# Rooms for the loads of "products down", and modulation rows, transposes and pairs of blocks further apart in a two-layer hybrid transformer step

## Chip, cores and metric

The kernel runs on one core of one Trainium2 chip. The metric is device time of one execution in microseconds, the median of the runs shown. The core's engines are PE (TensorE, matmuls and transposes), DVE (VectorE), ACT (ScalarE), POOL (GpSimd) and SP (SyncE, which here issues every DMA from one queue, in order). Each engine works through its own instructions in order and waits on semaphores where another engine or a DMA must have finished first.

## What is computed

One inference step of two layers over 1024 latent tokens and 128 context tokens, that is nine blocks of 128 tokens (0 to 7 latent, 8 the prompt), width 1024. Layer 0 has differential attention, layer 1 windowed attention with a sink; each is followed by a SwiGLU feed-forward of width 2816 = 22 x 128. Norms and modulation stand around each part:

```python
for i in range(DEPTH):
    mp = modulation(c_ctx[None, :], w_mod[i], b_mod[i])      # shift, scale, gate, twice, for the prompt
    ms = modulation(c, w_mod[i], b_mod[i])                   # and for the latent tokens
    hs = pre_norm_modulate(xs, norm_g[i, 0], ms[0], ms[1])
    ...                                                      # attention -> ys
    xs = post_norm_residual(xs, ys, norm_g[i, 1], ms[2])
    hs = pre_norm_modulate(xs, norm_g[i, 2], ms[3], ms[4])
    xs = post_norm_residual(xs, swiglu(hs, w_gate[i], w_up[i], w_down[i]), norm_g[i, 3], ms[5])
```

## The kernel before

Every product is made in three matmuls on values split into a high and a low part (hi x hi, hi x lo, lo x hi). So each weight and each activation is first split: ACT rounds it into the high part, DVE subtracts to get the low part.

A layer runs in stages: projections of q, k and v (`Qkv`), attention, output projection with the norms (`OProj`), "products up" (`Ffn.up`, the gate and up weights by a Strassen-like scheme in sums B11 to T4, accumulators X, Y and Z), and "products down" (`Ffn.downs`). After that comes the next layer's projection.

SBUF space is handed out as rooms of 128 x 1024 floats. `Rooms` is a list of free rooms: `take` removes the first, `give` appends at the end, and `retire` takes rooms out for good. A tile laid into a room waits until the reads and writes of the tile before it are done. H are 18 rooms on the left (h0 to h17), L nine more (ten in layer 1), D 18 on the right (d0 to d17). In layer 0 the rooms H become, pair by pair, the transposed input hT of layer 1's projections, two rooms per block.

Products down goes in steps (g, d): three groups g of three blocks, and 22 slices d of w_down, 66 steps in all, numbered 0 to 65 as loads. A step is 18 matmuls (dacc). `load_w` runs three steps ahead (lead = 3); in each step it takes five rooms and gives two back at once:

```python
x, a = rooms.take(name="fraw"), rooms.take(name="araw")
...
h, lo, ahl = [rooms.take((P, D), F32R, name) for name in ("fh", "fl", "ahl")]
...
rooms.give(x, a)
```

The three rooms of h, lo and ahl come back after the step's matmuls. For layer 0 the list starts as H[0:12], what is free of L and D[16:18]; at (0, 8) `retire(H)` takes all of H out of it. Beside the products, `mod_tasks_lean` makes modulation rows in these steps (DVE sums macc over eight pieces wmod of w_mod; then ACT and DVE split it to mhl; then `out()` has PE reduce it to a row, mrow, and DVE reads that row), and the blocks of the group before go through their norms (`norm`, parts 0 to 3 at d = 1 to 12), are stored to x_d, and are transposed (`turn`, at d = 12, 14, 16) into hT. In the last group the first projection weights of layer 1 (w2: wraw, split to whi and wlo) are loaded.

In products up, `mod_tasks_lean` runs in the same way between the products, and the mrow tile uses a "u" bank of PSUM, of which there are two; accumulator Z uses them too, for its two parts.

`pair` transposes two normed blocks xn on PE into the two "u" banks each (tp_n), copies the first (ACT B11h, B21h, DVE raw) and makes the sums from the second. Two pairs stand in `OProj` after block steps 5 and 6, the others in the first slice of products up, after products 0, 2 and 4 of part 0 (list `late`).

PE, DVE, ACT and POOL run in the order in which the code is written (`manual_schedule`); the order of DMAs on SP is set by a scheduler.

Of the kernel before, what the change touches and what calls it, by code (L numbers as in the profile page):

```python
# [18 lines left out]
P = 128  # L19
# [25 lines left out]
def hybrid_step(ctx: ExitStack, tc: tile.TileContext, x_prompt, x_sample, cache_diff_k, cache_diff_v,  # L45
# [201 lines left out]
    def mod_tasks_lean(ps, tasks, mroom, rooms, rows):  # L247

        out, n = None, 0
        for l, j, half in [(*t, half) for t in tasks for half in range(2)]:  # L250
# [3 lines left out]
            for kb in range(KB):  # L254
# [12 lines left out]
                if kb == 0 and out:  # L267
                    out()
# [1098 lines left out]
    class Halves:  # L1367
# [57 lines left out]
        def pair(self, part, c, xs, rooms):  # L1425

            raws, n = [], P if len(xs) == 2 else P // 2
            for i, x in enumerate(xs):
                tps = self.turned(x)
                if i == 0:  # L1430
                    raws.append(new(rooms[0], [P, 2, 4, n], F32, "raw"))
                    self.first(part, c, [tp[:, :, 0:n] for tp in tps], raws[0])
                if i == len(xs) - 1:
                    raws += [new(r, [P, 2, 4, n], F32, "raw") for r in rooms[1:]]
                    self.second(part, c, [tp[:, :, P - n:P] if n < P else tp for tp in tps], raws)

# [4 lines left out]
    class Ffn:  # L1441
# [127 lines left out]
        def up(self, tasks, mroom, late, pt, ahead):  # L1569

            self.pt = pt
            gen = mod_tasks_lean(self.ps, tasks, mroom, self.rooms, junk)
# [71 lines left out]
        def downs(self, mods, yx, hT, ahead=()):  # L1644
# [4 lines left out]
            for i, (g, d) in enumerate(steps):  # L1649
# [12 lines left out]
                if g:  # L1662
# [5 lines left out]
                    if self.l == 0 and d in (12, 14, 16):  # L1668
                        self.turn(GROUPS[g - 1][(d - 12) // 2])
# [3 lines left out]
                if g == 2 and d == 17:  # L1673
# [57 lines left out]
    class Layer:  # L1731
# [8 lines left out]
        def begin(self, stack):  # L1740
# [15 lines left out]
            def pair(part, c, *tbs):  # L1756
                rooms = [where[f"x{OORDER.index(tb) % 5}"] for tb in tbs]
                f.hv.pair(part, c, [op.xn[tb] for tb in tbs], [*rooms, *self.temps][:3])
                if part:
                    f.rooms.free += rooms  # L1760

            self.pair = pair
            for k, c, tbs in (((5, 1), 0, (0, 4)), ((6, 1), P, (1, 5))):
                hooks.setdefault(k, []).append(lambda c=c, tbs=tbs: pair(0, c, *tbs))
            hooks[5, 1].insert(0, lambda: f.hv.lay(0, iter(H)))
# [33 lines left out]
        def ffn(self, tasks):  # L1799

            l, f, op, H = self.l, self.f, self.op, self.H
            with ExitStack() as high:
# [3 lines left out]
                for tag in names:  # L1806
# [7 lines left out]
                late = [[lambda: self.pair(1, 0, 2, 6), lambda: f.fetch(1)], (), [lambda: self.pair(1, P, 3, 7)], (),  # L1814
                        [lambda: self.pair(1, 2 * P, TB_PROMPT)]]
# [10 lines left out]
        def down(self, stack, ahead=lambda ring: {}, tasks=()):  # L1826
# [4 lines left out]
            yx, cut = R[0:6], R[6:16] if l == 0 else R[6:8]  # L1831
# [3 lines left out]
            self.ring = Ring(cut[0:2], cut[2:] + rest + yx)  # L1835
            f.rooms.free += [r for r in self.old.free if r not in H] + rest
            steps = ahead(self.ring)
            if l == 0:

                steps.setdefault((0, 8), []).append(lambda: f.rooms.retire(H))  # L1840
                spare = Rooms(cut[4:6])
                gen = mod_tasks_lean(self.ps, tasks, [cut[0], *cut[1:4]], spare, new(cut[6]))
# [4 lines left out]
            self.low.close()  # L1847

# [144 lines left out]
```

## Time and profile before

| what | value |
|---|---|
| median of 3 runs | 3303.95 us (3297.66 to 3308.42) |
| the profiled execution's own time | 3303.71 us |
| its span, first to last instruction | 3301.9 us |
| mean granted TensorE clock | 0.969 |
| PE busy | 3038.3 us, 92% |
| DVE, ACT, POOL busy | 2023.9, 1423.1, 1359.9 us |

A share of busy time is an average over all stages; what ends a wait in one stage is read from the windows and waits of that stage. The granted clock is a share of full speed. "idle <- X" names what ended an engine's wait.

### The profile page before, as it was taken

Reading aid. Unit: us, or ns where it says so; the run is one execution under the profiler, and the core shown is the slowest. Engines: PE = TensorE matmul, PEld = TensorE weight load, DVE = VectorE, ACT = ScalarE, POOL = GpSimd, SP = SyncE. Lnnn points to the kernel's source line nnn. Section 1 sums busy time; section 2 is a strip of 40 time slices with the busy share of each in tenths; the row PEclk is TensorE's granted clock in tenths of the full one; section 3 lists DMA queues with packets and bytes.
Section 4 is the critical chain, followed back from the end, with each engine's and each line's share of the span. In section 5 each row is a group of like instructions: output and inputs, shape, how many; then the busy total and the mean of one; then the engine's idle time right before and its main releaser. Section 6 shows DMA issues by size and latency. Waiting matters only on the chain.

```text
span 3301.9 us, 47896 instructions
## 1 busy us (share of the span) xinstructions
PE 3038.3 (92%) x17998; PEld 2652.1 (80%) x17998; DVE 2023.9 (61%) x2789; ACT 1423.1 (43%) x2764; POOL 1359.9 (41%) x1186
## 2 busy tenths in 40 slices
PE   8999889888969999999868899899996999999999
PEld 5888777777758999998656678777776999998887
DVE  6776388887566777735563453799666733334454
ACT  6332267776543333333333422677444333333442
POOL 2543399997333434440010054466433433431001
PEclk9999999999989999999989899999998999999999
DMA  6765533332422333327454434443432422225564
GB/s 212 211 214 182 194 111 114 117 112 82 147 90 89 112 115 116 118 65 251 158 175 136 154 120 137 135 129 105 123 107 84 119 72 69 81 77 191 179 206 148
DMA packets 373808, 442.23 MB, mean 134 GB/s; under 512 B 26804, under 2 KB 295644, under 8 KB 373576
## 3 DMA queue, kind: packets, MB, share of 16 engines
q1 hardware_dynamic: 373576, 439.16, 42.4%
q8 instruction: 142, 2.33, 0.3%
q14 instruction: 90, 0.74, 0.1%
HBM read 335.71 MB, written 103.37 MB: 133 GB/s over the span
## 4 chain that ended last, share of the span: by engine, by line
PE 40%; DVE 8%; DMA 5%; ACT 4%; issue 1%; POOL 1%; ACTq 0%; SPq 0%; DVEq 0%; POOLq 0%
DMA fraw<-in_w_down_dram 5%; PE guX L1516 4%; PE guX L1518 4%; PE guX L1517 4%; PE dacc L1633 3%; PE dacc L1634 3%; PE dacc L1635 3%; DVE fl L1618 2%; PE guY L1518 2%; PE guY L1516 2%; PE guY L1517 2%; ACT fh L1617 2%; PE qacc L555 1%; PE qacc L556 1%; PE qacc L557 1%
## 5 line engine op out<-in xcount | busy, mean ns | idle before, releaser
L1633 PE MATMUL dacc<-fh,ahl 128*128 128x512 f32 x792 | 320.4, 405 | 24.5 <-ACT ahl L1619 14.6
L1618 DVE TENSOR_TENSOR fl<-fraw,fh 128x1024 fp32r<-128x1024 f32 x132 | 168.1, 1274 | 251.9 <-ACT fh L1617 251.8
L1634 PE MATMUL dacc<-fl,ahl 128*128 128x512 f32 x792 | 317.9, 401 | 3.6 <-DVE fl L1618 3.5
L1635 PE MATMUL dacc<-fh,ahl 128*128 128x512 f32 x792 | 317.5, 401 | 0.0
L1549 POOL TENSOR_TENSOR sg<-sg,U 128x256 f32<-128x256 f32 x88 | 75.0, 852 | 573.7 <-ACT sg L1548 558.4
L1617 ACT CAST fh<-fraw 128x1024 fp32r<-128x1024 f32 x132 | 138.4, 1049 | 339.4 <-DMA fraw<-in_w_down_dram 324.4
L154 POOL TENSOR_TENSOR xt<-yacc,xt 128x1024 f32<-128x1024 f32 (+1 forms) x19 | 46.3, 2439 | 534.6 <-DVE yacc L153 282.3
L555 PE MATMUL qacc<-whi,hh 128*128 128x512 f32 x648 | 261.5, 404 | 0.9 <-ACT hh L430 0.9
L556 PE MATMUL qacc<-wlo,hh 128*128 128x512 f32 x648 | 255.8, 395 | 0.0
L557 PE MATMUL qacc<-whi,hl 128*128 128x512 f32 x648 | 255.8, 395 | 0.0
L783 POOL TENSOR_TENSOR aT<-a,aT 128x512 fp32r<-128x512 f32 x186 | 240.1, 1291 | 15.5
L743 DVE TENSOR_REDUCE nm<-S 128x1 f32<-128x1280 f32 x128 | 190.3, 1486 | 50.4 <-PE S L736 50.1
L1633 PEld LDWEIGHTS dacc<-fh,ahl 128*128 128x128 f32 x792 | 153.1, 193 | 65.5 <-ACT ahl L1619 20.4
L736 PE MATMUL S<-K,q 128*128 128x512 f32 (+1 forms) x768 | 182.4, 373 | 12.8 <-ACT e L748 8.6
L1634 PEld LDWEIGHTS dacc<-fl,ahl 128*128 128x128 f32 x792 | 152.9, 193 | 41.5 <-DVE fl L1618 8.1
L265 DVE SCALAR_TENSOR_TENSOR macc<-wmod,sc,macc 128x512 f32<-128x512 f32 x196 | 184.2, 983 | 1.0 <-DMA wmod<-in_w_mod_dram 1.0
L1635 PEld LDWEIGHTS dacc<-fh,ahl 128*128 128x128 f32 x792 | 152.6, 193 | 38.5 <-DVE ahl L1620 4.0
L748 ACT ACTIVATE e<-S,nm 128x1280 f32<-128x1280 f32 x128 | 171.5, 1340 | 4.5 <-DVE nm L743 4.5
L577 ACT CAST xT<-tpx 128x512 fp32r<-128x512 f32 x127 | 68.4, 591 | 239.2 <-issue 125.3
L736 PEld LDWEIGHTS S<-K,q 128*128 128x128 f32 x768 | 135.7, 190 | 43.4 <-ACT e L748 19.1
L1488 DVE TENSOR_TENSOR fl<-fsum,fh 128x1024 fp32r<-128x1024 f32 x84 | 102.6, 1221 | 99.3 <-ACT fh L1486 99.3
L110 POOL TENSOR_SCALAR aT<-a 128x512 fp32r<-128x512 f32 x192 | 152.3, 793 | 21.8 <-ACT a L772 21.8
(369 smaller groups left out, 9710.7 us busy)
## 6 DMA issues: line engine op xcount, KB each, us to landing
fraw<-in_w_down_dram SPq DMA_DIRECT2D x132, 512.0 KB
wmod<-in_w_mod_dram SPq DMA_DIRECT2D x112, 256.0 KB
araw<-a_d SPq DMA_DIRECT2D x132, 192.0 KB
fraw<-in_w_gate_dram SPq DMA_DIRECT2D x44, 512.0 KB
fraw<-in_w_up_dram SPq DMA_DIRECT2D x42, 512.0 KB
qT_d<-xT SPq DMA_DIRECT2D x36, 512.0 KB
q<-qT_d SPq DMA_DIRECT2D x64, 256.0 KB
wraw<-in_w_qkv_diff_dram SPq DMA_DIRECT2D x24, 512.0 KB
```

The lines of the kernel that those rows point to most:

```text
L555: pe.matmul(acc, lhsT=xh, rhs=hi[:, a, :], start=(kb == 0), stop=False)
L556: pe.matmul(acc, lhsT=xh, rhs=lo[:, a, :], start=False, stop=False)
L557: pe.matmul(acc, lhsT=xl, rhs=hi[:, a, :], start=False, stop=(kb == KB - 1))
L736: pe.matmul(S[:, j:j + n], lhsT=self.q[:, f, m, i * P:(i + 1) * P], rhs=kv[self.h][0][:, m, j:j + n], start=(f == 0), stop=(f == 1))
L783: (dve if self.last else pool).tensor_tensor(out=lo, in0=x, in1=hi.bitcast(F32), op=ALU.subtract)
L1516: pe.matmul(o, lhsT=hi[:, kb, :], rhs=xh[:, kb, :], start=(first and kb == 0), stop=False, **more)
L1517: pe.matmul(o, lhsT=hi[:, kb, :], rhs=xl[:, kb, :], start=False, stop=False, **more)
L1617: act.copy(out=h, in_=x)
L1618: dve.tensor_tensor(out=lo, in0=x, in1=h.bitcast(F32), op=ALU.subtract)
L1633: pe.matmul(acc, lhsT=ah, rhs=hi[:, cs], start=(d == 0), stop=False)
L1634: pe.matmul(acc, lhsT=ah, rhs=lo[:, cs], start=False, stop=False)
L1635: pe.matmul(acc, lhsT=al, rhs=hi[:, cs], start=False, stop=(d == NDF - 1))
```

## The change

It has five parts, in the diff's order. `mod_tasks_lean` gets a number, lag: `out()` of one half row comes after piece lag of the next half instead of piece 0 (1 in products up, 3 in products down). `Halves.pair` becomes a generator that pauses after each block; in `OProj` its two halves come after the first and the second half projection of steps 5 and 6 (before, both after the second), and in the first slice of products up after products 1, 2, 3, 4 and 6. The turns move from d = 12, 14, 16 to 15, 17, 19, and the prompt's modulation rows from (2, 17) to (2, 20). Two rooms of D go from the ring of the next weights to the loads; the ring's raw rooms are H[15:17] during the stage and those two D rooms after it. H[0:6] are retired at (1, 12) and H[6:12] at (2, 4), in place of all H at (0, 8).

```diff
--- before.py
+++ after.py
@@ -244,7 +244,8 @@
             rows_out(l, j, half * 512, 512, r, *pre)
             yield
 
-    def mod_tasks_lean(ps, tasks, mroom, rooms, rows):
+    def mod_tasks_lean(ps, tasks, mroom, rooms, rows, lag):
+
 
         out, n = None, 0
         for l, j, half in [(*t, half) for t in tasks for half in range(2)]:
@@ -264,7 +265,7 @@
                     else:
                         dve.scalar_tensor_tensor(out=a, in0=w, scalar=sc[:, kb, cd:cd + 1], in1=a, op0=ALU.mult,
                                                  op1=ALU.add)
-                if kb == 0 and out:
+                if kb == lag and out:
                     out()
                 yield
             pre = rows_in(iter([rows[0:2, i * 512:(i + 1) * 512] for i in range(2)]), l, j, half * 512, 512)
@@ -1433,6 +1434,7 @@
                 if i == len(xs) - 1:
                     raws += [new(r, [P, 2, 4, n], F32, "raw") for r in rooms[1:]]
                     self.second(part, c, [tp[:, :, P - n:P] if n < P else tp for tp in tps], raws)
+                yield
 
 
 
@@ -1569,7 +1571,7 @@
         def up(self, tasks, mroom, late, pt, ahead):
 
             self.pt = pt
-            gen = mod_tasks_lean(self.ps, tasks, mroom, self.rooms, junk)
+            gen = mod_tasks_lean(self.ps, tasks, mroom, self.rooms, junk, 1)
             for d in range(NDF):
                 if d == 0:
 
@@ -1665,12 +1667,12 @@
                         part, j = [int(x) for x in NORMS[d - 1]]
                         if part < 2 or self.l == 0:
                             self.norm(part, GROUPS[g - 1][j])
-                    if self.l == 0 and d in (12, 14, 16):
-                        self.turn(GROUPS[g - 1][(d - 12) // 2])
+                    if self.l == 0 and d in (15, 17, 19):
+                        self.turn(GROUPS[g - 1][(d - 15) // 2])
                 if d == 17:
                     for j in range(3):
                         self.load_x(GROUPS[g][j], j)
-                if g == 2 and d == 17:
+                if g == 2 and d == NDF - 2:
                     self.mod(TB_PROMPT)
             for j in range(3):
                 for d in range(NDF - self.nlast, NDF):
@@ -1755,14 +1757,17 @@
 
             def pair(part, c, *tbs):
                 rooms = [where[f"x{OORDER.index(tb) % 5}"] for tb in tbs]
-                f.hv.pair(part, c, [op.xn[tb] for tb in tbs], [*rooms, *self.temps][:3])
+                yield from f.hv.pair(part, c, [op.xn[tb] for tb in tbs], [*rooms, *self.temps][:3])
                 if part:
                     f.rooms.free += rooms
+                yield
 
             self.pair = pair
-            for k, c, tbs in (((5, 1), 0, (0, 4)), ((6, 1), P, (1, 5))):
-                hooks.setdefault(k, []).append(lambda c=c, tbs=tbs: pair(0, c, *tbs))
-            hooks[5, 1].insert(0, lambda: f.hv.lay(0, iter(H)))
+            hooks.setdefault((5, 0), []).append(lambda: f.hv.lay(0, iter(H)))
+            for i, c, tbs in ((5, 0, (0, 4)), (6, P, (1, 5))):
+                steps = pair(0, c, *tbs)
+                for half in range(2):
+                    hooks.setdefault((i, half), []).append(lambda steps=steps, n=1 + half: step(steps, n))
 
             def room(tag, shape, dt, name):
                 return new(where[tag], shape, dt, name)
@@ -1811,8 +1816,9 @@
                 R.tile([P, 512], F32, name="room", tag="mw", bufs=2)
                 self.temps = [macc, (R, "mw", 2)]
                 pt = high.enter_context(sbuf(f"pt{l}", "right"))
-                late = [[lambda: self.pair(1, 0, 2, 6), lambda: f.fetch(1)], (), [lambda: self.pair(1, P, 3, 7)], (),
-                        [lambda: self.pair(1, 2 * P, TB_PROMPT)]]
+                pairs = [self.pair(1, c, *tbs) for c, tbs in ((0, (2, 6)), (P, (3, 7)), (2 * P, (TB_PROMPT,)))]
+                late = [[], [lambda: step(pairs[0])], [lambda: step(pairs[0], 2), lambda: f.fetch(1)],
+                        [lambda: step(pairs[1])], [lambda: step(pairs[1], 2)], [], [lambda: step(pairs[2], 2)]]
 
                 def switch():
 
@@ -1828,23 +1834,25 @@
 
             l, f, H = self.l, self.f, self.H
             R = ring_rooms(stack.enter_context(sbuf(f"D{l}", "right")), [f"d{i}" for i in range(18)])
-            yx, cut = R[0:6], R[6:16] if l == 0 else R[6:8]
+            yx, cut = R[0:6], R[6:14] if l == 0 else R[6:8]
             mods = [H[12:15], H[15:18]] if l == 0 else [cut[0:1], cut[1:2]]
             hT = alloc_hT(H) if l == 0 else None
             rest = [r for r in R[6:] if r not in cut]
-            self.ring = Ring(cut[0:2], cut[2:] + rest + yx)
+            self.ring = Ring(H[15:17], cut + rest[2:] + yx)
             f.rooms.free += [r for r in self.old.free if r not in H] + rest
             steps = ahead(self.ring)
             if l == 0:
 
-                steps.setdefault((0, 8), []).append(lambda: f.rooms.retire(H))
+                steps.setdefault((1, 12), []).append(lambda: f.rooms.retire(H[0:6]))
+                steps.setdefault((2, 4), []).append(lambda: f.rooms.retire(H[6:12]))
                 spare = Rooms(cut[4:6])
-                gen = mod_tasks_lean(self.ps, tasks, [cut[0], *cut[1:4]], spare, new(cut[6]))
+                gen = mod_tasks_lean(self.ps, tasks, [cut[0], *cut[1:4]], spare, new(cut[6]), 3)
                 for i in range(2 * NDF):
                     steps.setdefault(divmod(i, NDF), []).append(lambda: next(gen, None))
             with tc.manual_schedule(engines=ENGINES):
                 f.downs(mods, yx, hT, steps)
             self.low.close()
+            self.ring.rooms = rest[0:2], self.ring.rooms[1]
 
     before0, before1 = ExitStack(), ExitStack()
     with psum("gp0") as ps, sbuf("hT0", "left") as hp, sbuf("wq0", "left") as wq:
```

Three places show how instructions stand. First SP's queue in the last group of layer 0's products down (w_down into fraw, the a values into araw, stores to x_d), with the semaphores that each DMA waits for. Before:

```order
L1715 DMA x_d<-xt 128x1024 [waits Pool_49]
L1614 DMA fraw<-in_w_down_dram 128x1024 [waits DMAHW2_49,DVE_49]
L1615 DMA araw<-a_d 128x384 [waits DMAHW6_49,DMAHW3_49,DVE_49]
L1614 DMA fraw<-in_w_down_dram 128x1024 [waits DMAHW5_49,DVE_49]
L1615 DMA araw<-a_d 128x384 [waits DMAHW6_49,DVE_49]
```

And now:

```order
L1717 DMA x_d<-xt 128x1024 [waits DMAHW2_49,Pool_49]
L1616 DMA fraw<-in_w_down_dram 128x1024 [waits DMAHW3_49,PE_49]
L1617 DMA araw<-a_d 128x384 [waits DMAHW4_49,DVE_49,PE_49]
L1616 DMA fraw<-in_w_down_dram 128x1024 [waits DMAHW5_49,DVE_49,PE_49]
L1617 DMA araw<-a_d 128x384 [waits DMAHW6_49,DVE_49,PE_49]
```

The load of w_down waited for DVE alone (its room was last a raw tile, which DVE read); now it waits for PE too (its room was last a split weight).

Second, PE in products up of layer 0 (guX, guZ and guY are the accumulators, mrow the modulation row). Before:

```order
L1516 MATMUL guX<-B11h,fh 128x320
L1517 MATMUL guX<-B11l,fh 128x320
L1518 MATMUL guX<-B11h,fl 128x320
L279 MATMUL mrow<-mhl,sel 2x512 x4
L1516 MATMUL guZ<-B21h,fh 128x256
L1517 MATMUL guZ<-B21l,fh 128x256
```

And now:

```order
L1518 MATMUL guX<-T2h,fh 128x320
L1519 MATMUL guX<-T2l,fh 128x320
L1520 MATMUL guX<-T2h,fl 128x320
L280 MATMUL mrow<-mhl,sel 2x512 x4
L1518 MATMUL guY<-T3h,fh 128x256
L1519 MATMUL guY<-T3l,fh 128x256
```

The row's four matmuls moved from just ahead of Z to behind the second X product, ahead of Y.

Third, DVE in step 5 of layer 0's output projection (xn are normed blocks, L137 the reciprocal root of the norm, tp_n the transposed block, raw its copy). Before:

```order
L137 RECIPROCAL rs<-ss 128x1
L153 SCALAR_TENSOR_TENSOR xn<-oacc,rs,q 128x512 x2
L137 RECIPROCAL rs<-ss 128x1
L145 SCALAR_TENSOR_TENSOR xn<-K,rs,bc 128x1024
L146 TENSOR_TENSOR xn<-xn,bc 128x1024
L1395 COPY raw<-tp_n 128x512 x2
L1411 TENSOR_TENSOR raw<-tp_n,raw 128x512
```

And now:

```order
L1396 COPY raw<-tp_n 128x512 x2
L1278 RECIPROCAL rs_9227<-ss_9161 128x8
L1279 TENSOR_TENSOR rs_9227<-rs_9227,r_9160 128x8
L137 RECIPROCAL rs<-ss 128x1
L153 SCALAR_TENSOR_TENSOR xn<-oacc,rs,q 128x512 x2
L137 RECIPROCAL rs<-ss 128x1
L145 SCALAR_TENSOR_TENSOR xn<-K,rs,bc 128x1024
L146 TENSOR_TENSOR xn<-xn,bc 128x1024
L1412 TENSOR_TENSOR raw<-tp_n,raw 128x512
```

The copies of the pair's first block moved ahead of the norm of block step 4; the sums with the second block stay behind it.

## Rows read from the trace of the kernel before

**Rows 1.** The page: busy time of PE, and the chain's shares by line.

```profile
PE 3038.3 (92%) x17998; PEld 2652.1 (80%) x17998; DVE 2023.9 (61%) x2789; ACT 1423.1 (43%) x2764; POOL 1359.9 (41%) x1186
...
DMA fraw<-in_w_down_dram 5%; PE guX L1516 4%; PE guX L1518 4%; PE guX L1517 4%; PE dacc L1633 3%; PE dacc L1634 3%; PE dacc L1635 3%; DVE fl L1618 2%; PE guY L1518 2%; PE guY L1516 2%; PE guY L1517 2%; ACT fh L1617 2%; PE qacc L555 1%; PE qacc L556 1%; PE qacc L557 1%
```

**Rows 2.** Windows: us, busy PE PEld DVE ACT POOL, clock, DMA share, GB/s.

```profile
1512.60:1571.40 58.80, 58.36 (x265) 47.90 (x264) 40.12 (x55) 22.29 (x31) 2.68 (x2) 1.00 0.76 258
1571.40:1894.80 323.40, 259.17 (x1015) 196.24 (x1014) 159.04 (x200) 110.48 (x171) 28.64 (x12) 0.89 0.48 156
3050.00:3250.00 200.00, 200.00 (x871) 163.11 (x870) 105.36 (x114) 80.18 (x121) 19.58 (x6) 1.00 0.63 206
1670.00:1720.00 50.00, 35.70 (x142) 26.53 (x142) 34.26 (x41) 16.59 (x28) 10.20 (x5) 0.89 0.61 199
```

**Rows 3.** Windows of tile dacc alone, busy PE PEld DVE ACT.

```profile
1512.60:1571.40 58.80, 54.20 (x235) 44.00 (x236) 0.00 (x0) 0.00 (x0) 1.00 0.76 258
1670.00:1720.00 50.00, 32.36 (x130) 24.47 (x129) 0.00 (x0) 0.00 (x0) 0.89 0.61 199
```

**Rows 4.** The chain in order of time, layer 0's products down: start, us, what.

```profile
1573.78 3.51 DMA fraw<-in_w_down_dram
1577.37 1.06 ACT fh L1617
1578.45 1.24 DVE fl L1618
...
1877.97 3.53 DMA fraw<-in_w_down_dram
```

**Rows 5.** Waits of SP's queue, 1571.4 to 1894.8: total, times, longest.

```profile
SPq L1614 <- DVE fl L1618: 125.7, 50, 7.2
```

**Rows 6.** Waits of PE, 1571.4 to 1894.8.

```profile
PE mrow L279 <- ACT mhl L272: 18.5, 3, 7.8
PE dacc L1633 <- ACT ahl L1619: 14.6, 13, 3.4
PE tp_n L162 <- POOL yacc L146: 13.1, 2, 7.2
```

**Rows 7.** Timeline of PE: a turn in the projections of layer 1.

```profile
1917.90 1.06 PE L162 MATMUL tp_n<-ident,yacc 128*128 128x128 f32 x8
```

**Rows 8.** Timeline of all engines near 1700.

```profile
1700.19 2.35 POOL L146 TENSOR_TENSOR yacc<-yacc,bc 128x1024 f32<-128x1024 f32 x1 [22.70 <-DVE yacc L145]
...
1701.56 2.06 DVE L1618 TENSOR_TENSOR fl<-fraw,fh 128x1024 fp32r<-128x1024 f32 x1 [1.45 <-ACT fh L1617]
```

**Rows 9.** Waits of PE in products up: layer 0 to 1270, to 1515; layer 1.

```profile
PE guZ L1516 <- DVE junk L203: 5.9, 5, 1.2
...
PE guZ L1516 <- DVE junk L203: 2.4, 2, 1.2
...
PE guZ L1516 <- DVE junk L203: 1.2, 1, 1.2
```

**Rows 10.** Waits of PE around the pairs: 890 to 1030, 2400 to 2540.

```profile
PE tp_n L1387 <- DVE raw L1395: 22.9, 4, 11.2
...
PE tp_n L1387 <- DVE raw L1395: 19.7, 4, 10.6
```

**Rows 11.** Timelines of DVE and PE around the pairs of layer 1.

```profile
2435.26 0.16 DVE L137 RECIPROCAL rs<-ss 128x1 f32<-128x1 f32 x1 [4.02 <-ACT ss L135]
...
2440.16 0.69 DVE L1411 TENSOR_TENSOR raw<-tp_n,raw 128x512 f32<-128x512 f32 x1 [0.89 <-PE tp_n L1387]
...
2460.75 0.69 DVE L1411 TENSOR_TENSOR raw<-tp_n,raw 128x512 f32<-128x512 f32 x1 [1.47 <-PE tp_n L1387]
...
2490.42 0.58 PE L1518 MATMUL guX<-B11h,fl 128*128 128x256 f32 x1 [4.72 <-DVE fl L1488]
```

**Rows 12.** Timelines of SP and DVE at the start of layer 1's projections.

```profile
1893.68 0.33 SPq L540 DMA_DIRECT2D cos<-in_rope_cos_dram  x1
...
1900.99 0.42 DVE L607 TENSOR_TENSOR t<-qacc,cos 128x256 f32<-128x256 f32 x1
```

## The prediction

> **What bounds the kernel now.** I read the page first: PE is busy 3038 of 3302 us, so 264 us is all that waiting costs in the whole kernel, and the chain that ended last runs mostly over PE, except for one DMA line, the loads of w_down, with 5%, and DVE fl with 2% [rows 1]. Two layers have the same "products down" stage, so I laid their windows side by side [rows 2]. In layer 1 PE is busy 200.00 of 200 us at clock 1.00; 871 matmuls there make 0.2296 us each, 4.13 us for a step of 18 (a few records may be missing, which would make the pace a little faster). In layer 0 the first 58.8 us look the same (58.36 busy, clock 1.00), and then the stage falls apart: 323.4 us with 259.2 busy at clock 0.89. The stage is thus lost after its first 14 steps, not at its start.
>
> The chain in order of time says to what: a load of 3.51 us, the cast to fh of 1.06, the subtraction to fl of 1.24, and at once the next load [rows 4]. From the load at 1573.78 to the one at 1877.97 there are 50 such rounds (loads 15 to 65), 304.2 / 50 = 6.08 us each, against 4.13 us of PE work. The queue's own waits agree: SP held the w_down load for DVE fl 50 times, 125.7 us [rows 5]. The code says why. A step takes five rooms (fraw, araw, fh, fl, ahl) and gives two back at once; three steps run ahead and hold nine. After (0, 8) the list is 11 rooms: nine of L and two of D. The list is first in, first out, so after a load it holds two rooms, the step just multiplied adds three behind them, and fraw always gets the room that the load before it has just left. Eleven rooms are one raw buffer.
>
> **The change part by part.**
>
> *Rooms.* After the change the list has 9 + 4 + 12 = 25 rooms up to (1, 12), then 19, and 13 from (2, 4) on. Going through the list by hand: with 25 rooms load i gets the room of araw of load i-4; with 19, once the held rooms have drained, that of fh of step i-5; with 13 that of fl of step i-4 (two loads at each turnover get the raw room of the load two or three before). None is the room of load i-1, so no load waits for the split just ahead of it. With 13 rooms the path after a room comes free is 3.51 + 1.06 + 1.24 and hand-overs, about 5.9 us [rows 4], while PE has three steps, 12.4 us, between the products of i-4 and those of i. So PE's pace should hold to the end. The first 14 steps of before are direct evidence that it holds with modulation loads beside it: they ran so at 258 GB/s and a DMA share of 0.76 [rows 2].
>
> The price: 235 dacc matmuls lie in the first window [rows 3], so 1188 - 235 = 953 remain, 953 x 0.2296 = 218.8 us; six turns at 1.06 us when nothing stops them [rows 7] are 6.4; twelve modulation matmuls x 0.23 are 2.8. Together 228.0 us, against 323.4: 95.4 us to be had, and that is one end. The other end is nothing (the loads stay serial for another reason). I keep 8 us of stalls, about a sixth of the 46 us that PE waits there for mrow, ahl and the turns [rows 6], since group ends and in-order waits for a norm's root stay. **-88 us.** The low clock of 0.89 is no term of its own: at layer 1's pace the clock is 1.00 in the same matmuls.
>
> *Turns at 15, 17, 19 and modulation rows with lag 3.* These are waits inside that stage: 13.1 us for POOL yacc before the turns and 18.5 us for ACT mhl before mrow [rows 6]; they are in the 95.4 already. They are needed with it: at 4.13 us a step the old distance of two steps from norm to turn would be 8 us, while POOL's sum alone takes 2.35 [rows 8]. The turned blocks are read only in the next stage, after PE has at least two steps left, so later costs nothing.
>
> *Modulation rows with lag 1 in the products up.* mrow's four matmuls stood just ahead of the two Z products, which need both "u" banks, so Z waited for DVE to read mrow: 5.9 + 2.4 + 1.2 us, eight times 1.2 [rows 9]. One step later mrow follows the T2 product, when Z has been read. **-9.5 us**, that or nothing; the mhl rooms are held two products longer, which the list, never empty, covers.
>
> *Pairs further apart.* PE waits 22.9 and 19.7 us for the copies of the raw blocks [rows 10]. If PE were the limit, 42.6 us would be the gain. It isn't. DVE is: in a paired step it stands 4.02 us waiting for the norm's root, then copies, and waits only 0.89 and 1.47 us for PE's second transposes; and PE, arriving at the first product up, still waits 4.72 us for DVE's fl [rows 11]. What PE saves earlier it waits there. DVE saves its own small waits, 2.4 us in the first two pairs, and something like 1 us in the late three, where Z now holds a "u" bank until DVE gets to it. -3 us a layer, **-6 us**; ends +4 (the late pairs lose what the early ones win) and -12.
>
> *Hand-over to the next layer's projections.* The raw rooms of w2 move from D to H, free early; two of its loads now stand ahead of most of the first w_down loads, but five mod_d loads stood there before and one of them goes later. The prompt's rows come at (2, 20) behind w2's splits; they are read only after the first projection (24 matmuls, 5.5 us), so nothing waits. But two 512 KB loads of the next weights now stand in SP's queue ahead of cos and sin, which went out at 1893.68 and were read at 1900.99 [rows 12]. I take **+1.5 us** of DVE delay, from 0 to +4.
>
> Sum, against the profiled execution's own 3303.7 us (the median shown is 3303.95, the same): 3303.7 - 88 - 9.5 - 6 + 1.5 = **3202 us**.
>
> **The rivals.**
>
> *DVE falls behind in the middle group.* Between 1670 and 1720 DVE was busy 34.26 us [rows 2] for 130 / 18 = 7.2 steps [rows 3], 4.75 us a step, more than PE's 4.13. Excess 0.62 x 7.2 = 4.5 us, within three steps of lead (12.4 us), so hidden. One of its subtractions took 2.06 us instead of 1.24 beside a POOL sum [rows 8]. If each of the six POOL sums of a group (2.35 us) stopped DVE for its whole length, 14.1 us come on top, 18.6 in all, 6.2 beyond the lead; in both later groups about 12 us: 3214. The Trainium skill has this as a rule (SBUF — State Buffer, "SBUF: two separate sides"): a VectorE instruction with two SBUF inputs and a GpSimd one take the shared port pair exclusively, and the loser waits for the whole instruction. The row above, in which DVE started 1.0 us before the end of POOL's sum and lost 0.8, agrees in kind. By the rule in full the sum would be this rival's.
>
> *The last group runs dry.* With 13 rooms the x_d stores, held in SP's queue for POOL, or the w2 loads keep the w_down loads back and they stay at 6.08 us: 14 loads from (2, 8) x 1.95 = 27 us: 3229. Against it: 6.5 us of slack per load.
>
> *The loads aren't freed.* SP's order, which a scheduler sets, or the DMA rate holds each load for the split ahead anyway; only the up stage and the pairs gain: 3303.7 - 14 = 3290. Against it the first 14 steps.
>
> *Slower: loads behind products.* The rooms that loads get now were last read by PE, not by DVE. Were such a room given back by step i-1, load and products would alternate: 4.13 + 5.9 = 10.0 us a step. From the first retirement's drain on (loads 41 to 65) that is 25 x 3.92 = +98, minus 26 x 1.95 = 51 gained before and 14 elsewhere: 3337. It decides as soon as the releasing step is less than two before the load's own; the list gives four.
>
> **How the numbers follow.** Forecast 0.65 (its own range 3190 to 3211); DVE behind 0.17 (3214); last group dry 0.09 (3229); loads not freed 0.05 (3290); slower 0.04 (3337). Taking in the stall allowance from 0 to 14 us, the pairs' ends and the first two rivals gives 3184 to 3236; outside lie the last two. About 0.3% (10 us) is what a measurement of this kernel can tell from no change. Slower by more is the last rival, 0.04; the case of 3290 is so near that bound that 0.02 of it counts as the same; faster 0.94.
>
> **What would show it.** In the changed trace: layer 0's stage from the first dacc to the first qacc near 295 us instead of 382, clock near 1.00, and the w_down loads off the chain; SP's waits for DVE fl gone. mrow and Z waits in the up stage at nothing. Between the pairs: PE's wait for raw gone, its wait at the first product longer by nearly as much, DVE's chain 2 to 3 us shorter. It is wrong if PE idles in g = 1 before fl (DVE), in g = 2 before fh with a DMA releaser (rooms), or if the first projections wait for cos.

## The result, and the profile after

The changed kernel takes 3199.9 us (median of 4 runs, 3196.25 to 3200.84) against 3301.59 us (4 runs): a ratio of 0.9688, 95% interval 0.9669 to 0.9707, 101.7 us less. The profiled execution took 3199.07 us, its span is 3197.3 us.

Laid out by the first start of each accumulator tile (oacc: output projection, guX: products up, dacc: products down, qacc: next projections), the spans compare so, in us:

| from, to | before | after | change | predicted |
|---|---|---|---|---|
| layer 0: first oacc, first guX | 145.5 | 139.1 | -6.4 | pairs -3, in this row and the next together |
| first guX, first dacc | 545.6 | 537.0 | -8.6 | lag 1: -8.3 |
| **first dacc, first qacc** | **382.2** | **298.1** | **-84.1** | **-88** |
| first qacc, first oacc of layer 1 | 457.5 | 456.1 | -1.4 | +1.5 |
| layer 1: first oacc, first guX | 133.0 | 130.5 | -2.5 | pairs -3, in this row and the next together |
| first guX, first dacc | 528.4 | 529.3 | +0.9 | lag 1: -1.2 |
| first dacc, end | 288.2 | 286.6 | -1.6 | 0 |

The page of the changed kernel: PE is 94% busy, and in the chain's shares by line, the second row, no DMA line is left, where the loads of w_down had 5% [rows 1].

```profile
PE 3001.8 (94%) x17998; PEld 2636.8 (82%) x17998; DVE 2048.6 (64%) x2789; ACT 1421.9 (44%) x2764; POOL 1361.9 (43%) x1186
...
POOL aT L784 7%; PE guX L1518 6%; PE guX L1519 6%; PE guX L1520 6%; PE dacc L1635 5%; PE dacc L1637 5%; PE dacc L1636 5%; POOL aT L110 4%; PE qacc L556 4%; PE qacc L558 4%; PE qacc L557 4%; PE guY L1518 3%; PE guY L1520 3%; PE guY L1519 3%; PE guZ L1518 1%
```

The windows of layer 0's products down, columns as in [rows 2]: the first 58.8 us, the rest, and the whole.

```profile
1496.70:1555.50 58.80, 58.36 (x265) 47.86 (x264) 42.36 (x58) 27.17 (x38) 2.78 (x2) 1.00 0.85 299
1555.50:1794.80 239.30, 230.48 (x1016) 186.67 (x1015) 169.59 (x197) 105.23 (x165) 35.80 (x12) 0.99 0.59 195
...
1496.70:1794.80 298.10, 288.84 (x1279) 234.54 (x1278) 211.95 (x255) 132.40 (x202) 38.58 (x14) 0.99 0.64 215
```

The 323.4 us of [rows 2] became 239.3 with all but the same instructions, and the clock is 0.99 instead of 0.89. Of SP's queue, from 1555.5 to 1794.8, the waits that answer to [rows 5]:

```profile
SPq L1617 <- PE dacc L1637: 58.1, 21, 8.1
...
SPq L1616 <- DVE ahl L1622: 19.5, 13, 3.8
...
SPq L1616 <- DVE fl L1620: 3.9, 3, 1.9
```

The load of w_down (now L1616) waited 50 times, 125.7 us, for the subtraction of the load ahead; now 3 times, 3.9 us. It also waits 13 times, 19.5 us, for DVE's ahl; by the list, with 25 rooms, that is the ahl of the load four back, whose araw had the room, and not that of the load ahead. Most of SP's waiting is now for PE's products, after which rooms come free. What PE itself still waits for in the stage, in place of [rows 6]:

```profile
PE tp_n L162 <- DVE hl L165: 4.7, 2, 4.3
PE mrow L280 <- DVE mhl L274: 4.1, 1, 4.1
PE dacc L1635 <- DVE U L1554: 0.4, 1, 0.4
```

All three name DVE, none a DMA. The forecast allowed 8 us there; 9.3 us of the window are idle (298.10 - 288.84). Why DVE is late shows in the timeline of DVE and POOL at the first norm of the middle group:

```profile
1613.10 1.22 DVE L1620 TENSOR_TENSOR fl<-fraw,fh 128x1024 fp32r<-128x1024 f32 x1
1613.32 3.27 POOL L154 TENSOR_TENSOR xt<-yacc,xt 128x1024 f32<-128x1024 f32 x1 [107.09 <-ACT ss L135]
1614.23 2.77 DVE L1622 TENSOR_TENSOR ahl<-araw,ahl 128x384 fp32r<-128x384 f32 x1
1616.93 0.87 DVE L264 TENSOR_SCALAR macc<-wmod,sc 128x512 f32<-128x512 f32 x2
```

POOL's sum starts while DVE's fl runs and lasts 3.27 us, 0.92 longer than the 2.35 of [rows 8], about what was left of fl. The ahl behind fl, 0.54 us elsewhere, lasts 2.77 and ends 0.4 us after POOL's sum. They run one after the other. A longer wait of DVE for POOL's results is not the reason: in the whole stage no wait of DVE names POOL; the longest in total are for ACT fh, 33.0 us, and for PE dacc, 17.2.

The late pairs of blocks did not get shorter, they wait elsewhere. PE's waits in layer 1 from 2290 to 2440, and the timeline of DVE and POOL just ahead of the longest:

```profile
PE guX L1519 <- DVE B11l L1409: 9.4, 1, 9.4
PE tp_n L1388 <- DVE raw L1396: 7.7, 3, 3.9
PE oacc L1326 <- DVE xn L153: 6.0, 1, 6.0
PE guX L1520 <- DVE fl L1490: 4.5, 1, 4.5
```

```profile
2422.70 1.32 POOL L1471 TENSOR_TENSOR fsum<-fsum,fraw 128x512 f32<-128x512 f32 x1
2422.83 1.48 DVE L1409 TENSOR_TENSOR T3l<-raw,T3h 128x256 fp32r<-128x256 f32 x1
...
2423.99 1.44 POOL L1476 TENSOR_TENSOR fsum<-fraw 128x512 f32<-128x512 f32 x1
2424.34 1.37 DVE L1421 TENSOR_TENSOR raw<-raw 128x256 f32<-128x256 f32 x1
...
2425.39 1.44 POOL L1477 TENSOR_TENSOR fsum<-fraw,fsum 128x512 f32<-128x512 f32 x1
2425.63 1.48 DVE L1409 TENSOR_TENSOR B11l<-raw,B11h 128x256 fp32r<-128x256 f32 x1
...
2427.04 0.41 DVE L1409 TENSOR_TENSOR B21l<-raw,B21h 128x256 fp32r<-128x256 f32 x1
```

DVE operations of this size take 0.41 us (the last row); beside POOL's sums for the next weights each takes 1.4 to 1.5, and PE stands 9.4 us for the third of them. By these three rows that is about 3 us of the 9.4; no run takes POOL's sums away here.

### The profile page after: what moved, and what is told of

Same layout as the page of the kernel before. It is cut to its first block, busy times and chain, and to the rows that moved or that the text cites. A ratio compares the mean times of both kernels' runs of the same rounds, so it can differ in the third digit from the quotient of the medians.

```text
span 3197.3 us, 47914 instructions
## 1 busy us (share of the span) xinstructions
PE 3001.8 (94%) x17998; PEld 2636.8 (82%) x17998; DVE 2048.6 (64%) x2789; ACT 1421.9 (44%) x2764; POOL 1361.9 (43%) x1186
## 4 chain that ended last, share of the span: by engine, by line
PE 67%; POOL 14%; DVE 9%; ACT 4%; issue 3%; DMA 2%; SPq 1%; DVEq 0%; ACTq 0%; POOLq 0%
POOL aT L784 7%; PE guX L1518 6%; PE guX L1519 6%; PE guX L1520 6%; PE dacc L1635 5%; PE dacc L1637 5%; PE dacc L1636 5%; POOL aT L110 4%; PE qacc L556 4%; PE qacc L558 4%; PE qacc L557 4%; PE guY L1518 3%; PE guY L1520 3%; PE guY L1519 3%; PE guZ L1518 1%
## 5 line engine op out<-in xcount | busy, mean ns | idle before, releaser
L1635 PE MATMUL dacc<-fh,ahl 128*128 128x512 f32 x792 | 312.0, 394 | 2.3 <-DVE U L1554 2.3
L1636 PE MATMUL dacc<-fl,ahl 128*128 128x512 f32 x792 | 310.7, 392 | 0.0
L1637 PE MATMUL dacc<-fh,ahl 128*128 128x512 f32 x792 | 310.7, 392 | 0.0
L737 PE MATMUL S<-K,q 128*128 128x512 f32 (+1 forms) x768 | 184.5, 377 | 12.9 <-ACT e L749 8.9
L1635 PEld LDWEIGHTS dacc<-fh,ahl 128*128 128x128 f32 x792 | 149.2, 188 | 36.4 <-DVE U L1554 3.1
L1637 PEld LDWEIGHTS dacc<-fh,ahl 128*128 128x128 f32 x792 | 149.0, 188 | 33.7
```

The source lines that it names most:

```text
L737: pe.matmul(S[:, j:j + n], lhsT=self.q[:, f, m, i * P:(i + 1) * P], rhs=kv[self.h][0][:, m, j:j + n], start=(f == 0), stop=(f == 1))
L1635: pe.matmul(acc, lhsT=ah, rhs=hi[:, cs], start=(d == 0), stop=False)
L1636: pe.matmul(acc, lhsT=ah, rhs=lo[:, cs], start=False, stop=False)
L1637: pe.matmul(acc, lhsT=al, rhs=hi[:, cs], start=False, stop=(d == NDF - 1))
```

## The experiments

Each was timed against the kernel before on the same chip, in three series: a, b1 to b4, and b5 with c. The kernel before took 3301.61, 3303.34 and 3301.09 us in them, so kernels of two series compare to some 2 us only. "The stage" is layer 0's products down, from the first dacc to the first qacc.

**The parts alone.** Four kernels: the changed one with lag 1 in products up and all pairs as before; the kernel before with lag 1 in products up only, and with the pairs only; and the changed one with the late pairs whole.

```diff
# a1_down_only (from the changed kernel; OProj's pairs whole too)
-gen = mod_tasks_lean(self.ps, tasks, mroom, self.rooms, junk, 1)
+gen = mod_tasks_lean(self.ps, tasks, mroom, self.rooms, junk, 0)
...
# a1_down_only and a4_late_whole
-late = [[], [lambda: step(pairs[0])], [lambda: step(pairs[0], 2), lambda: f.fetch(1)],
...
+late = [[lambda: drain(self.pair(1, 0, 2, 6)), lambda: f.fetch(1)], (), [lambda: drain(self.pair(1, P, 3, 7))], (),
+        [lambda: drain(self.pair(1, 2 * P, TB_PROMPT))]]
# a2_lag_up (from the kernel before; a3_pairs_only takes the pairs' hooks and list alone)
-if kb == 0 and out:
+if kb == lag and out:
```

> The stage 'products down' of layer 0 as changed (rooms, turns, modulation lag 3 there); the products up with lag 0 and all five pairs of blocks in one piece, as in the kernel before. Theory (the gain is made inside that stage, by loads that no longer get the room of the load ahead): the stage from first dacc to first qacc takes 296 to 300 us, as after the whole change, and the time is 3301.6 - 84 to 88, 3214 to 3218. PE's waits for mrow ahead of Z (9.5 us) and for raw between pairs (22.9 and 19.7 us) are all there again. Rival (the products up and the pairs earn part of what shows in the down stage, because a stage that starts at another time finds other loads): the stage takes 305 us or more, and the time is above 3222.

Measured: 3216.61 us, ratio 0.9744 (0.9729 to 0.9758), 85.0 us less; the stage took 300.1 us, the output projection and products up of layer 0 took 145.1 and 542.7, against 145.5 and 545.6 (more on these 2.9 us below). The theory holds: the stage earns its gain by itself.

> The kernel before with nothing but lag 1 in the products up. Theory (Z's wait for mrow's bank is on PE's path and the path is PE's alone there): minus 9.5 us, 3292, and the waits of guZ for DVE junk are gone. Rival (PE is held by something else a product later, such as DVE fl or the T sums): 3299 to 3303, with PE waits of about 1 us each at another line.

Measured: 3288.72 us, ratio 0.9961 (0.9949 to 0.9974), 12.9 us less, more than the 9.5 of the waits. In layer 0's products up, from 1030 us on, PE has one wait left, and none for mrow's bank:

```profile
PE guX L1516 <- ACT U L1541: 0.5, 1, 0.5
```

First guX to first dacc went from 545.6 to 532.6 us. But 2.8 of these 13.0 us were won in the first slice, ahead of the first row: it took 61.3 us at a granted clock of 0.78 before, and 58.5 at 0.85 here. Kernels that do the same there have either length (58.4 in a1_down_only, 61.5 in b1_lead2), and in layer 1 it went the other way, from 58.4 to 60.9. Behind the first slice it is 484.3 against 474.1 us, at a clock of 1.00 in both: 10.2 us for seven waits. PE's timeline around one of them in the kernel before shows why it is more than 1.19 each:

```profile
1078.31 0.28 PE L1517 MATMUL guZ<-B21l,fh 128*128 128x256 f32 x1
1078.42 0.28 PE L1518 MATMUL guZ<-B21h,fl 128*128 128x256 f32 x1
1079.89 0.42 PE L1516 MATMUL guZ<-B21h,fh 128*128 128x320 f32 x1 [1.19 <-DVE junk L203]
1080.15 0.31 PE L1517 MATMUL guZ<-B21l,fh 128*128 128x320 f32 x1
1080.30 0.31 PE L1518 MATMUL guZ<-B21h,fl 128*128 128x320 f32 x1
```

Running, a product of 256 starts 0.12 us behind the one ahead, one of 320 0.15. Around the wait the starts are 1.47 and 0.26 apart, so 1.35 + 0.11 = 1.46 us are lost where the idle column says 1.19: the matmul's tail, which overlaps the next one otherwise, is counted as busy. Seven times 1.46 is the 10.2 us of layer 0. With the one in layer 1 it is 11.7 us, within the interval of the 12.9; the rest is not resolved.

> The kernel before with nothing but the pairs of blocks apart (in the output projection and in the first slice of products up). Theory of the prediction: minus 3 us in each layer, 3295.6. Rival that the trace of the changed kernel suggests: layer 0 gains 6 to 7 us and layer 1 under 1 us, because there the late pairs give back at PE's wait for B11l what the early ones win; the sum is nearly the same, 3294 to 3296, but first oacc to first dacc is 684 us instead of 691 in layer 0 and 661 instead of 661.4 in layer 1.

Measured: 3295.44 us, ratio 0.9983 (0.9974 to 0.9992), 6.2 us less. By stretches: output projection -6.3 and -3.1 us, first guX to first dacc +1.5 and +3.8. Early pairs win, late pairs give some of it back. How much is not known well: the late pairs stand in the first slice of products up, which differs by 2.5 to 3 us between executions of the same code. In layer 0 PE's wait for B11l is 9.4 us there too.

> The changed kernel, but the three late pairs in one piece after products 0, 2 and 4 of part 0, as before; the two pairs in the output projection stay apart. Theory (DVE's chain is the limit, the early pairs shorten it, and the late pairs apart lose since Z holds a bank until DVE gets to it, so that DVE then comes to B11l 9.4 us late in both layers): 3 to 6 us less than the changed kernel, 3194 to 3197, and PE's wait for B11l after the late pairs falls below 3 us. Rival (the late pairs apart are what gains): 3 to 6 us more, 3203 to 3206, with raw waits of about 10 us in each layer.

Measured: 3199.62 us, ratio 0.9693 (0.9679 to 0.9706): no difference from the changed kernel that these runs resolve. PE's waits in layer 1 from 2240 to 2480:

```profile
PE tp_n L1388 <- DVE raw L1396: 12.5, 3, 11.2
PE oacc L1326 <- DVE xn L153: 6.0, 1, 6.0
PE guX L1520 <- DVE fl L1490: 4.6, 1, 4.6
PE guX L1518 <- ACT U L1543: 3.5, 2, 2.8
...
PE guX L1519 <- DVE B11l L1409: 1.4, 1, 1.4
```

B11l fell from 9.4 to 1.4 as expected, but raw rose from 7.7 to 12.5 and guX's wait for ACT U from 0.5 to 3.5. The theory, 3 to 6 us less, is not borne out: where the late pairs stand does not matter within 5 us. That DVE has the same work either way would explain it; no run shows that this is the reason. Products up are 1.8 and 2.5 us shorter in this trace, no more than the first slice differs by itself.

**Which room, or how many.** The kernel before with loads two steps ahead in layer 0; and the changed kernel with H retired where it was before, so 13 rooms from (0, 8).

```diff
# b1_lead2 (from the kernel before)
-self.lead, self.nlast = 3, 3 + l
+self.lead, self.nlast = 2 + l, 3 + l
# b2_retire_early (from the changed kernel)
-steps.setdefault((1, 12), []).append(lambda: f.rooms.retire(H[0:6]))
-steps.setdefault((2, 4), []).append(lambda: f.rooms.retire(H[6:12]))
+steps.setdefault((0, 8), []).append(lambda: f.rooms.retire(H))
```

> The kernel before, with one number changed: in layer 0 the loads of products down run two steps ahead instead of three. No room is added: the list has 11 rooms after (0, 8). Two steps hold six of them, and by the list the load of step i then gets the room of fh of step i-3, not that of the load ahead. Theory (the serial chain comes from which room a load gets, not from how many rooms there are): the loads no longer wait for DVE fl of the load ahead; a room comes free at the start of step i-2 and the path of 5.9 us fits in two steps, 8.3 us, with 2.4 us to spare, so the stage takes 300 to 325 us instead of 382 and the time is 3220 to 3245, with less looking ahead than before. Rival (11 rooms are too few, and the looking ahead is what counts): the stage is as long as before or longer, 382 us and up, the time 3300 to 3340.

Measured: 3243.88 us, ratio 0.9822 (0.9805 to 0.9838): 59.5 us less with no room added and less looking ahead. The stage's window, and SP's waits in it from 1571.4 on:

```profile
1511.90:1834.90 323.00, 301.09 (x1278) 237.75 (x1278) 213.10 (x255) 132.56 (x202) 35.68 (x14) 0.96 0.62 204
```

```profile
SPq L1615 <- PE dacc L1635: 80.7, 31, 5.6
SPq L258 <- DVE macc L265: 34.0, 14, 5.1
```

The wait of L1614 for DVE fl is gone. So it was which room a load gets that made the loads serial. Its stage is still 25 us longer than the changed kernel's. That has the shorter lead, fewer rooms and the old turns and lag in it, which this run does not take apart; one part that shows is the modulation loads (L258), held 34.0 us for DVE macc in SP's queue with w_down loads behind them.

> The changed kernel, but all rooms H leave the list at (0, 8), as before: it has 13 rooms from there on (nine of L, four of D) instead of 25 and 19. By the list load i then gets the room of fl of step i-4 all along. Theory (any room but that of the load ahead will do): no slower than the changed kernel by more than 5 us, 3198 to 3205; the 12 rooms lent until their turn are worth nothing here, the two more of D are the change. Rival (more rooms let loads run further ahead, past the group ends and DVE's slow stretches): 10 to 30 us more, 3210 to 3230, with PE waits for fh or ahl in the middle group.

Measured: 3213.67 us, ratio 0.9733 (0.9719 to 0.9748), 13.8 us more than the changed kernel (12.0 when each is taken from the kernel before of its own series); the stage took 311.3 us. The theory said at most 5: any room but the last is not enough by itself. PE's waits in the stage:

```profile
PE tp_n L162 <- DVE hl L165: 5.8, 2, 4.4
PE mrow L280 <- ACT mhl L273: 5.0, 1, 5.0
PE mrow L280 <- DVE mhl L274: 4.7, 1, 4.7
PE dacc L1637 <- DVE ahl L1622: 2.0, 1, 2.0
```

The rival named the price rightly, not the place: PE waits for the modulation row's split more than for fh or ahl.

**Turns and lag in products down.**

```diff
# b3_turns_early (from the changed kernel); c1_rooms_alone is this and lag 0 in products down (the prompt's rows stay at (2, 20) in both)
-if self.l == 0 and d in (15, 17, 19):
+if self.l == 0 and d in (12, 14, 16):
...
-steps.setdefault((1, 12), []).append(lambda: f.rooms.retire(H[0:6]))
-steps.setdefault((2, 4), []).append(lambda: f.rooms.retire(H[6:12]))
+steps.setdefault((1, 9), []).append(lambda: f.rooms.retire(H[0:6]))
+steps.setdefault((2, 1), []).append(lambda: f.rooms.retire(H[6:12]))
# b5_old_rooms (from the changed kernel; also retire(H) at (0, 8) and the prompt's rows at (2, 17), both as before)
-yx, cut = R[0:6], R[6:14] if l == 0 else R[6:8]
+yx, cut = R[0:6], R[6:16] if l == 0 else R[6:8]
...
-self.ring = Ring(H[15:17], cut + rest[2:] + yx)
+self.ring = Ring(cut[0:2], cut[2:] + rest + yx)
```

> The changed kernel, but the turns at d = 12, 14, 16 as before, and the rooms retired three steps earlier for it, at (1, 9) and (2, 1). Theory of the prediction (at 4.13 us a step the old distance of two steps is too short, with POOL's sum of 3.3 us and DVE's own work between): PE waits for POOL yacc or DVE hl at the turns, 5 to 13 us in all, 3205 to 3213. Rival (the distance is enough, two steps are 8.3 us): 3198 to 3202.

Measured: 3197.93 us, ratio 0.9684 (0.967 to 0.9699); stage 295.4 us, no wait at the turns. The rival holds.

> The changed kernel with the turns at d = 12, 14, 16 (rooms retired three steps earlier for it) and lag 0 in products down, both as before: of the down stage only the rooms are changed. Theory (the rooms are the whole gain of that stage; turns and lag only move waits that PE does not have once the loads run ahead): the stage takes 295 to 300 us, the time is 3196 to 3203. Rival (the prediction's: at 4.13 us a step the modulation row needs its distance): PE waits for DVE mhl before each of four rows, 8 to 15 us, the time is 3206 to 3215.

Measured: 3198.45 us, ratio 0.9689 (0.9673 to 0.9705); stage 296.1 us. The rooms (with the prompt's rows, which stay late) are the whole gain of the stage. PE waited once for DVE mhl, 4.0 us, as with lag 3.

> The changed kernel with the rooms, the ring and retire(H) at (0, 8) as before; turns at 15, 17, 19, lag 3 in products down, lag 1 in products up and the pairs apart stay. Theory (turns and lag give nothing while the loads are serial, since PE waits for the next load instead): the stage is 378 to 384 us, the time 3301.6 - 12.9 - 6.2, 3279 to 3286. Rival (PE's waits for mrow and at the turns, 18.5 and 13.1 us in the kernel before, are on the path even there): the stage is 360 us or less, the time below 3265.

Measured: 3278.78 us, ratio 0.9931 (0.9916 to 0.9946); stage 376.1 us, both just under the theory's ranges and far from the rival's. SP's wait is back (128.6 us over the same stage in the kernel before):

```profile
SPq L1616 <- DVE fl L1620: 118.8, 52, 3.8
```

Without the rooms, turns and lag give 6 us of the 84.

**Why DVE is late.**

```diff
# b4_sums_dve (from the changed kernel); the same for pre_norm
-post_norm([y], rstd(self.ss[tb]), m[0], x, x, y)
+post_norm([y], rstd(self.ss[tb]), m[0], x, x, y, self.eng(tb))
...
+def eng(self, tb):
+    return pool if self.l or tb in GROUPS[2] else dve
# c3_13_rooms_dve: b4_sums_dve with b2's retire; c4_sums_dve_both: b4_sums_dve and
-post_norm(self.acc[tb], rs, gg, x, x, self.xn[tb], dve if OORDER.index(tb) < 2 else pool)
+post_norm(self.acc[tb], rs, gg, x, x, self.xn[tb], dve)
```

> The changed kernel, but the twelve sums with two 128x1024 operands in the norms of layer 0's products down, groups 0 and 1, run on DVE instead of POOL. In the changed kernel POOL takes 3.3 us for one, and the DVE ahl beside it 2.75 us instead of 0.54. Theory (DVE loses in each the 2.2 us that the two engines keep each other out; alone on DVE the sum costs 1.2): DVE's busy time in the middle and last groups falls or stays, every ahl takes 0.54 us, PE's wait for mrow (4.1 us) and at the turns (4.7) go down, and the time is 0 to 6 us less, 3194 to 3200. Rival (the slow ahl has another reason, such as DMA traffic): ahl stays at 2.75 us and DVE has 14 us more work, 3200 to 3210.

Measured: 3189.85 us, ratio 0.9659 (0.9644 to 0.9674), 10 us less than the changed kernel by the medians (11.8 within the series). The two intervals touch, but the stage resolves it, 287.2 us against 298.1. Its window, and DVE in it:

```profile
1500.70:1787.90 287.20, 285.81 (x1278) 232.61 (x1278) 206.28 (x267) 133.28 (x202) 2.81 (x2) 1.00 0.67 224
```

```profile
1615.83 1.28 DVE L153 SCALAR_TENSOR_TENSOR yacc<-yacc,rs,bc 128x1024 f32<-128x1024 f32 x1
1617.15 1.22 DVE L154 TENSOR_TENSOR xt<-yacc,xt 128x1024 f32<-128x1024 f32 x1
1618.29 1.22 DVE L1620 TENSOR_TENSOR fl<-fraw,fh 128x1024 fp32r<-128x1024 f32 x1
1619.43 0.55 DVE L1622 TENSOR_TENSOR ahl<-araw,ahl 128x384 fp32r<-128x384 f32 x1
```

DVE does 12 instructions more (x267 against x255) and is busy 5.7 us less (206.28 against 211.95). Twelve sums at 1.22 us are 14.6 us, so the other operations of DVE lost some 20 us less. PE's idle time in the stage fell from 9.3 to 1.4 us, its busy time by 3.0 at clock 1.00 instead of 0.99. The theory holds; its bound of 6 us was too low.

> 13 rooms from (0, 8) on and the twelve sums of the norms on DVE instead of POOL, together. Alone, 13 rooms cost 13.8 us against the changed kernel and the sums on DVE gained 10. Theory (the lent rooms only bridge the stretches in which DVE falls behind; without those, 13 rooms are enough): 3189 to 3194, as with the sums on DVE alone, the stage 287 to 291 us. Rival (the number of rooms counts for itself, because with few of them the modulation loads, which wait for DVE macc, hold the w_down loads behind them in SP's queue): 3200 to 3206.

Measured: 3195.36 us, ratio 0.968 (0.9665 to 0.9694); stage 294.7 us. The time lies between the two ranges. With the sums on POOL, 13 rooms cost 13.8 us; with them on DVE, 5.5 (by the stages 13.2 and 7.5, within the series 12.0 and 7.8). So a part of what the lent rooms are worth, between a third and 60%, is bridging DVE's stretched operations. The rest fits the rival: SP held modulation loads 47.0 us for DVE macc, against 13.0 in b4_sums_dve, and PE waited 5.7 us for the row.

```profile
SPq L259 <- DVE macc L266: 47.0, 21, 4.1
```

> The kernel with the twelve sums on DVE, and also the sums of the output projection's post norms (L154, seven a layer on POOL) on DVE. On POOL one takes 2.38 us, on DVE 1.22; DVE waits 4.01 us behind it for the norm's root, so DVE's chain from one norm to the next gets shorter by 1.16 us and no other work of DVE is kept waiting. Theory (that chain sets the pace of the paired steps and of the first slice of products up): 7 x 1.16 = 8 us at most in each layer, less where PE sets the pace: 6 to 14 us less than 3189.9, 3176 to 3184. Rival (PE's projections or POOL's rounding set the pace there, or DVE's lower parts come later): no change, 3187 to 3192.

Measured: 3174.09 us, ratio 0.9615 (0.9601 to 0.963): faster than both kernels, 15.8 us below b4_sums_dve by the medians, 13.5 when each is taken from the kernel before of its own series; the upper end was 14. The norm's chain in layer 1's output projection, first of the changed kernel, then of this one:

```profile
2330.04 1.41 DVE L153 SCALAR_TENSOR_TENSOR xn<-oacc,rs,bc 128x512 f32<-128x512 f32 x2
2331.53 2.38 POOL L154 TENSOR_TENSOR q<-xn,q 128x1024 f32<-128x1024 f32 x1 [5.07 <-DVE xn L153]
...
2335.46 0.17 DVE L137 RECIPROCAL rs<-ss 128x1 f32<-128x1 f32 x1 [4.01 <-ACT ss L135]
```

```profile
2311.83 1.41 DVE L153 SCALAR_TENSOR_TENSOR xn<-oacc,rs,bc 128x512 f32<-128x512 f32 x2
2313.28 1.23 DVE L154 TENSOR_TENSOR q<-xn,q 128x1024 f32<-128x1024 f32 x1
2316.11 0.16 DVE L137 RECIPROCAL rs<-ss 128x1 f32<-128x1 f32 x1 [1.60 <-ACT ss L135]
```

From L153 to L137 it is 5.42 us there and 4.28 here, 1.14 less; if all seven norms in each of two layers are like this one, that makes 16.0 us. DVE's chain sets the pace in these stretches: what shortens it shows in the time. Stretched operations are not what was won here: DVE's busy time in the whole kernel rose from 2043.6 to 2061.8 us, by 18.2, and 14 sums at 1.22 are 17.1.

## Why the prediction was right, and where it was not

**The bound and the rooms: right, -88 against -84.1 in the stage and -85.0 alone.** The loads were serial because each got the room of the load ahead; one number that changes which room comes up (b1_lead2) took 59.5 us off without a room, and the old rooms brought SP's 118.8 us wait back (b5_old_rooms). The pace of layer 1 was the right yardstick: without stalls the terms gave 58.8 + 228.0 = 286.8 us for the stage, and b4_sums_dve, nearly without stalls, took 287.2.

**The 8 us of stalls: size right, cause wrong.** They were put down to group ends and waits for a norm's root. They were the first rival's mechanism: DVE and POOL keeping each other out, 10.9 us of the stage (298.1 - 287.2). That rival put 12 us on top of the 8; in fact it was nearly all there is. With the sums on DVE, group ends and waits for a root are still there, and PE idles 1.4 us. The Trainium skill (SBUF — State Buffer, "SBUF: two separate sides") calls the port pair that these two engines share an exclusive lock, held for the whole instruction. The trace agrees in both directions: POOL's sum lost the 0.9 us that fl had left, ahl lost the 2.2 that POOL then had. But not every such loss reached PE: DVE lost some 20 us in the stage and PE 10.9, and with fewer rooms (b2_retire_early) PE lost more.

**Turns and lag in products down "needed with it": wrong.** At 4.13 us a step the old distances are enough (b3_turns_early, c1_rooms_alone). The prediction's own figures said so: two steps are 8 us, and the sum that has to fit in them took 2.35.

**Lag 1 in products up: right, mis-sized, -9.5 against -12.9.** The term took the idle time of a wait, 1.19 us; from start to start it costs 1.46, 11.7 for the eight. The last 1.2 of the 12.9 are not resolved.

**The pairs: -6 against -6.2 alone, right by luck.** Taken was 2.4 us won in the early pairs of a layer and about 1 in the late three. The early ones won 6.3 and 3.1 us, and the late ones lost 1.5 and 3.8 (each to some 3 us): wins and losses that were not forecast made nearly the forecast sum. PE's wait for raw, which was to be gone, fell from 22.9 to 10.1 us and from 19.7 to 7.7. PE's wait at the first product, which should have grown by nearly what was saved, went from 5.2 to 7.4 us in layer 0 and not at all in layer 1; the new wait is at B11l.

**The hand-over: +1.5 against nothing that shows.** The stretch is 1.4 us shorter, and in the traces of the other runs it takes 455.4 to 458.4 us. Cos went out 0.4 us after the first qacc instead of 1.1 before, and was read 6.1 us after it, against 6.2.

The remaining rivals fell: the last group does not run dry (PE busy 92.11 of the last 96.8 us, no wait with a DMA releaser), and no load of w_down has to wait for the split or the products of the step just ahead: by the list, worked through by hand, the room is that of a load four or more back, save two loads at each turnover. The parts measured alone add up to 85.0 + 12.9 + 6.2 = 104.1 us, the whole is 101.7; the difference is within the intervals. The total, 3199.9 against 3202, is closer than its parts: the stage brought 4 us less than forecast, lag 1 some 2 to 3 us more.

## What to carry to other kernels

Where buffers come from a first-in, first-out list, work out whose buffer each load gets: a list that just suffices can turn a lead of three into one buffer, and a shorter lead can be faster than a longer one. Before splitting work between DVE and POOL, add what the two take from each other: a sum that took POOL 2.35 us cost DVE 2.2 us of a neighbour, and 1.22 us when DVE did it itself. A repeated short stall of PE is priced from start to start, not by the idle column.

## What was not expected of the hardware

A 1.19 us wait of PE cost 1.46 us, since the wait counts only from the end of the matmul ahead, which otherwise overlaps the next (starts at 1078.42 and 1079.89, 0.28 us each, and 0.12 apart without a wait). Stalls cost again through the clock: between the changed kernel and b4_sums_dve, 7.9 us less idle time in the stage came with 3.0 us less busy time for the same matmuls, at a granted clock of 1.00 instead of 0.99. In the changed kernel the clock was 0.75 from 1661 to 1666 us and 0.70 from 1780 to 1785, right behind PE's two long waits of 4.13 and 4.33 us, and 1.00 in the 5 us after each. A part of the 3.0 us, not measured here, are tails of matmuls before a wait. And moving twelve instructions onto the busier engine lowered its busy time by 5.7 us.
